# A hybrid decoder layer: the first head pair's half projections as three per attention step, and the memory's 1/rms operations at a higher priority

## The chip, the cores and the metric

The kernel runs on one core of a Trainium2 chip. The metric is device time in microseconds of one execution, as the median of several runs. The engines named below are PE (the matrix engine, with PEld for its weight loads), DVE (the vector engine), ACT (the scalar engine), POOL (the general engine) and SP (which here only issues DMA transfers).

## The reference

One layer of a causal decoder is computed for a batch of 1, 512 tokens and a model width of 1024, in float32. Only the mixer sublayer's attention and the memory's RMSNorm matter here:

```python
h = rms_norm(x, norm_mix[l])
proj = h @ w_in[l]
q_a, k_a, v_a, u_b, gate_b, gate_c, g_a, g_b = jnp.split(proj, split_points, axis=-1)
...
z = jnp.einsum('bhqd,bhkd->bhqk', qb, kb) * scale
log_fail = jnp.where(mask, jax.nn.log_sigmoid(-z), 0.0)
log_later = lax.cumsum(log_fail, axis=3, reverse=True) - log_fail
weights = jnp.where(mask, jnp.exp(jax.nn.log_sigmoid(z) + log_later), 0.0)
outs.append(jnp.einsum('bhqk,bhkd->bhqd', weights, vb))
...
y_b = gate_b * causal_depthwise_conv(gate_c * u_b, conv_w[l])
merged = jax.nn.sigmoid(g_a) * branch_a + jax.nn.sigmoid(g_b) * branch_b
x = x + merged @ w_mix_out[l]
x = x + memory_cross_attention(rms_norm(x, norm_mem_q[l]), rms_norm(mem, norm_mem_kv[l]), ...)
```

The stick-breaking attention has 8 heads of 64 channels. A weight of key s for query t is a sigmoid times a product over the keys between them, so each score tile needs a sum over all later keys before its exponential can be taken. After the mixer come the cross-attention into 256 memory tokens, a SwiGLU sublayer and a last RMSNorm.

## The kernel before, in words

Every float32 operand of a matmul is split into a high part, rounded to the matmul's own format, and a low part. A product takes three matmuls: high by high, high by low, low by high (`mm3`, lines 155 to 157). A weight tile is loaded by SP (`wr`, line 143), cast by ACT to its high part (`wh`, line 150) and subtracted by DVE to its low part (`wl`, line 151). There are four buffers each of `wr`, `wh` and `wl`.

The input projection is computed in column blocks of 128. One block is a projection of 8 chunks of the model width, 24 matmuls of 128x512 into one PSUM bank `pr`. It is cut in two halves of 12 matmuls each, `open_project` and the rest in `project`, and after the second half DVE evicts the bank: `qk_part` for queries and keys (L294), `conv` for the convolution branch (`gc` L315, `cu` L321 and L322, `cv` L324 and L328, `gb` L334 and L335) and `gate` for the merge gates (L307). The pool of these banks (`pmm`) has two.

The attention works on pairs of heads p = 0 to 3, and for each pair on key tiles kt = 3, 2, 1, 0, each with all queries from its own on. That makes 16 steps, numbered 0 to 15 in the text, with 128, 256, 384 and 512 queries for two heads. For one step

- `scores` makes z = q.k on PE (L382 or L389), then ACT takes |z|, exp and log (L396 to L398), DVE adds max(z, 0) to make e (L399), and POOL clears what lies above the diagonal (L355);
- `parts` adds on DVE the carry, the sum over later tiles (L420), and splits e into high and low, `l`, by ACT (L369) and DVE (L370);
- `weights` adds with PE the running sum of both parts onto z by a triangular matrix (`negtri`, L433); then DVE takes the next carry from row 0 of z (L438), which SP copies from partition 0 to partition 127 (L444), ACT takes the exponential `a` (L441), POOL clears its diagonal block, and DVE splits it into `ah` and `al` (L449, L450);
- `values` multiplies by v on PE (L461).

The loop over steps runs one step ahead with the scores: iteration i computes some half projections, then the scores of step i+1, then `weights` of step i, which wait for the second `l` of step i, and then `values` of step i-1. So the half projections of an iteration are the work on PE under which ACT, DVE and POOL bring z of step i to `l`. How many of the 44 halves an iteration takes is set by the table `FILL`: its first row gives the shares of pair 0's four steps, its second row those of each other pair, and `fill_some` takes halves until the cumulated share is reached. The order of the 44 is fixed: queries and keys of the next pair, then gc, u and gb of the convolution, pair by pair, and at the end four merge gates. Before, the shares sum to 44, so the iterations take 3, 2, 3, 3 halves and then 2, 2, 3, 4 for each of the other three pairs.

The order of PE's work is the order of the code. On ACT, DVE, POOL and SP a list scheduler sets the order at build time by the code's order and by priorities: `tc.high_priority(n)` lets the operations inside it count as written n places earlier. The attention's own chain uses 100 and 150.

The squares of the memory are summed on the way. In iteration 14 two small products with a constant (`var`, L188, ahead of the scores; `varb`, L197, after the values) give its mean square by token and along the free axis, each in a bank of `pmm`, and `rstd_of` makes 1/rms of each, `rm` and `rmb`, with operations on ACT (L121, L126, L127) and DVE (L124, L128, L129, L131). They are needed much later, at `km` and `vm`.

Of the kernel before, what the change touches and what calls it, by code (L numbers as in the profile page):

```python
# [29 lines left out]
MEM_AT = (5, 7, 9, 11)  # L30
MEAN_AT = 14
EARLY = 2
FILL = ((3, 2, 3, 3), (2, 2, 3, 4))
WARM = 8
FIRST = 4

# [4 lines left out]
def hybrid_layer(ctx: ExitStack, tc: tile.TileContext, xT_d, memT_d, cols_d, wv_d, win_d,  # L41
# [135 lines left out]
    def squares_mean(acc, n):  # L177

        parts = unit("acch", n * P), unit("accl", n * P)
        nc.vector.tensor_copy(parts[0], acc)  # L180
        nc.vector.tensor_tensor(out=parts[1], in0=acc, in1=f(parts[0]), op=ALU.subtract)

        def by_token(s, tables=(), bank=otile):

            vp = bank("var")
            for t in range(n):
                for i in range(2):
                    nc.tensor.matmul(vp[:, 2 * t:2 * t + 2], parts[i][:, t * P:(t + 1) * P],  # L188
                                     mean_r[:, 0:2], start=i == 0, stop=i == 1)
            return rstd_of(vp[:, 0:2 * n].rearrange("p (t two) -> p t two", two=2)[:, :, 0], n, s,  # L190
                           tables)

        def along(s, tables=(), bank=otile, keep=None):

            vp = bank("varb")[:, :n * P]
            for i in range(2):
                nc.tensor.matmul(vp, mean_r, parts[i], start=i == 0, stop=i == 1)  # L197
            return rstd_of(vp, n * P, s, tables, keep=keep)

        return by_token, along  # L200
# [103 lines left out]
    def gate(m, j):  # L304
        ps = project((O_A, O_B)[j] + m * P)
        t = gates[m, j] = tmp("g")
        nc.vector.tensor_tensor(out=t, in0=ps, in1=r0b, op=ALU.mult)  # L307
# [65 lines left out]
    def scores(p, kt):  # L373
        c0, n = span(kt)
        q, k = qk[p]
        ks = slice(kt * P, (kt + 1) * P)
        terms = (0, 0), (0, 1), (1, 0)
        if 2 * n <= 512:
            zs[p, kt] = [ztile("z")[:, :2 * n]]
            z3 = by_head(zs[p, kt], kt)[0]  # L380
            for i, (a, b) in enumerate(terms):
                nc.tensor.matmul(z3, k[a][:, ks], late_q[p % 2][b][:, :, c0 - HS:],  # L382
                                 start=i == 0, stop=i == 2)
        else:
            zs[p, kt] = [ztile("z")[:, :n] for _ in range(2)]
            for i, (a, b) in enumerate(terms):
                for h in range(2):
                    hs = slice(h * HD, (h + 1) * HD)
                    nc.tensor.matmul(zs[p, kt][h], k[a][hs, ks], q[b][hs, c0:],  # L389
                                     start=i == 0, stop=i == 2)  # L390
        es[p, kt] = []
        with tc.high_priority(100):
            for h, z in enumerate(zs[p, kt]):
                w = z.shape[1]
                e = tmp("e")[:, :w]
                nc.scalar.activation(e, z, AF.Abs)  # L396
                nc.scalar.activation(e, e, AF.Exp, scale=-1.0)
                nc.scalar.activation(e, e, AF.Ln, bias=1.0)  # L398
                nc.vector.scalar_tensor_tensor(out=e, in0=z, scalar=0.0, in1=e, op0=ALU.max,  # L399
                                               op1=ALU.add)  # L400
                causal(by_head([e], kt)[0])
                es[p, kt].append(e)
                if kt > 0:
                    r = carries[kt % 2][0:1, h * w:(h + 1) * w]
                    first.setdefault((p, kt), []).append(r)
                    nc.scalar.copy(r, z[0:1, :])

    def parts(p, kt):


        c0, n = span(kt)
        sp[p, kt] = []
        with tc.high_priority(100):
            for h, e in enumerate(es.pop((p, kt))):
                w = e.shape[1]
                if kt < TT - 1:
                    c = carries[(kt + 1) % 2][P - 32:P, h * w // n * (n - P):]
                    c = c[:, :w // n * (n - P)].rearrange("p (h n) -> p h n", n=n - P)
                    e3 = e.rearrange("p (h n) -> p h n", n=n)[P - 32:P, :, P:]
                    nc.vector.tensor_tensor(out=e3, in0=e3, in1=c, op=ALU.add)  # L420
                sp[p, kt].append(lsplit(e, w, f"l{kt % 2}"))
# [6 lines left out]
    def weights(p, kt):  # L428
        c0, n = span(kt)
        av[p, kt] = []  # L430
        for z, both in zip(zs[p, kt], sp[p, kt]):
            for part in both:
                nc.tensor.matmul(z, negtri, part, start=False, stop=True, skip_group_check=True)  # L433
        exp_a = []
        got = first.get((p, kt), [])
        with tc.high_priority(150):
            for r, z in zip(got, zs[p, kt]):
                nc.vector.tensor_tensor(out=r, in0=r, in1=z[0:1, :], op=ALU.subtract)  # L438
            for h, z in enumerate(zs[p, kt]):
                exp_a.append(tmp("a")[:, :z.shape[1]])  # L440
                exps.append(nc.scalar.activation(exp_a[h], z, AF.Exp))  # L441
            for h, r in enumerate(got):
                w = r.shape[1]
                nc.sync.dma_start(carries[kt % 2][P - 1:P, h * w:(h + 1) * w], r)  # L444
        for a in exp_a:
            causal(by_head([a], kt)[0])
            w = a.shape[1]
            ah, al = unit("ah")[:, :w], unit("al")[:, :w]
            nc.vector.tensor_copy(ah, a)  # L449
            nc.vector.tensor_tensor(out=al, in0=a, in1=f(ah), op=ALU.subtract)  # L450
            for i in range(w // n):
                av[p, kt].append((ah[:, i * n:(i + 1) * n], al[:, i * n:(i + 1) * n]))

    def values(p, kt):
        c0 = span(kt)[0]
        if kt == TT - 1:
            ops[p] = [otile("o") for _ in range(2)]
        for h in range(2):
            w = v[kt][h][:, p, :, :]
            for i in range(2):  # L460
                nc.tensor.matmul(ops[p][h][:, c0:], w, av[p, kt][h][i],  # L461
                                 start=kt == TT - 1 and i == 0, stop=kt == 0 and i == 1,
                                 skip_group_check=True)
        if kt == 0:

            t = tmp("ot")
            for h in range(2):
                hs, other = (slice(j * HD, (j + 1) * HD) for j in (h, 1 - h))
                nc.scalar.copy(t[hs, :], ops[p][h][other, :])
                nc.vector.tensor_tensor(out=t[hs, :], in0=ops[p][h][hs, :], in1=t[hs, :],  # L470
                                        op=ALU.add)
            oT.append(split(t, "o"))
# [7 lines left out]
    def mem_square(k2):  # L480

        mk = f(unit("mk")).rearrange("p (j t) -> p j t", j=2)
        load_mem(k2, mk)
        nc.scalar.activation(accm if k2 == 0 else mk, mk, AF.Square)
        if k2 > 0:
            nc.vector.tensor_tensor(out=accm, in0=accm, in1=mk, op=ALU.add)
        if k2 == KD // 2 - 1:
            nc.vector.tensor_tensor(out=accm[:, 0, :], in0=accm[:, 0, :], in1=accm[:, 1, :],
                                    op=ALU.add)
# [16 lines left out]
    n_fill = len(fill)  # L506
    shares = FILL[0] + (TT - 1) * FILL[1]

    def fill_some(to):
        while fill and n_fill - len(fill) < to:  # L510
            g, *args = fill.pop(0)
            g(*args)
# [5 lines left out]
    with tc.manual_schedule(engines={mybir.EngineType.PE}):  # L518
        for i in range(len(steps) + 1):
            if i in MEM_AT:  # L520
                mem_square(MEM_AT.index(i))
            if i == MEAN_AT - 2:
                mean = squares_mean(accm[:, 0, :], MT)
            fill_some(n_fill * sum(shares[:i + 1]) / sum(shares))
            if i == MEAN_AT:
                rm = mean[0]("rm", bank=mmtile)
            if i + 1 < len(steps):
                scores(*steps[i + 1])
            if i < len(steps):
                weights(*steps[i])  # L530
            else:
                gate(EARLY, 0)
            if i + 1 < len(steps):
                parts(*steps[i + 1])
            if i > 0:
                values(*steps[i - 1])
            if i == MEAN_AT:
                rmb = mean[1]("rmb", bank=mmtile)

    stick.close()  # L540
    xpool = ctx.enter_context(tc.tile_pool(name="xpool", bufs=8))
# [552 lines left out]
```

## Time and profile before

| | us |
|---|---|
| median of 3 runs | 861.33 |
| lowest and highest of them | 860.83, 861.85 |
| the profiled execution's own time | 860.98 |
| its span | 859.2 |
| PE busy | 850.5 |
| DVE busy | 586.5 |
| ACT busy | 431.1 |
| POOL busy | 62.0 |

Times in rows are counted from the span's start. A row of the timeline gives the start, the duration, the engine, the line, the operation, out<-in and how many instructions are merged; in brackets stands how long the engine had been idle before and what released it. Matmuls overlap in the pipeline, so a 128x512 one shows a duration of about 0.39 us while the next starts some 0.23 us after it; lengths of PE's work are therefore taken from start to start. The same is done for DVE, whose rows overlap by under 0.1 us.

### The profile page before, as it was taken

The page shows a single profiled execution, that of the slowest core. Times are in us where ns is not written, and L with a number is a line of the kernel's source. Part 1 is how long each engine was busy: PE and PEld are TensorE (multiplying, and loading weights), DVE is VectorE, ACT ScalarE, POOL GpSimd, SP SyncE. Part 2 cuts the span into 40 slices and gives each one's busy share as a digit, 9 for nine tenths or more (in the row PEclk, how much of TensorE's full clock was granted, in tenths as well). Part 3 has the DMA queues.
Part 4 walks back from the last instruction along what each step waited for, and adds up shares of the span by engine and source line. Part 5 has one row for each costly group of instructions (what it writes and reads, how often), then busy time and mean ns, then how long its engine had stood idle before and what let it go on. Part 6 is the DMA issues. An engine that isn't in the chain of part 4 may idle for free.

```text
span 859.2 us, 12693 instructions
## 1 busy us (share of the span) xinstructions
PE 850.5 (99%) x4912; PEld 748.6 (87%) x4912; DVE 586.5 (68%) x963; ACT 431.1 (50%) x750; POOL 62.0 (7%) x92
## 2 busy tenths in 40 slices
PE   9999999999999999999999999999999999999997
PEld 7877788888888898888888889999999999888897
DVE  8769898986454475555555779888887778533334
ACT  7566766665333344433444666555445556422335
POOL 1011111111000000000000101111111100000002
PEclk9999999999999999999999999999999999999999
DMA  8322331228333255422110527776777753322202
GB/s 295 132 90 77 120 111 62 74 99 266 111 103 111 96 177 184 143 98 98 50 67 33 137 54 202 187 182 172 185 188 195 182 147 127 119 98 99 73 1 98
DMA packets 42859, 108.34 MB, mean 126 GB/s; under 512 B 4656, under 2 KB 8752, under 8 KB 42800
## 3 DMA queue, kind: packets, MB, share of 16 engines
q1 hardware_dynamic: 36528, 95.72, 32.8%
q0 software_dynamic: 5984, 11.54, 8.2%
q8 instruction: 38, 0.62, 0.3%
q10 hardware_dynamic: 288, 0.29, 0.1%
q14 instruction: 21, 0.17, 0.1%
HBM read 104.36 MB, written 2.10 MB: 124 GB/s over the span
## 4 chain that ended last, share of the span: by engine, by line
PE 96%; DVE 2%; DMA 1%; issue 0%; POOL 0%; SPq 0%; DVEq 0%; ACT 0%; POOLq 0%
PE z L801 15%; PE y L801 7%; PE pr L155 7%; PE pr L156 7%; PE pr L157 7%; PE f L156 5%; PE f L157 5%; PE f L155 5%; PE v L801 4%; PE r L156 3%; PE r L155 3%; PE r L157 3%; PE v L261 3%; PE mq L156 2%; PE mq L157 2%; PE mq L155 2%
## 5 line engine op out<-in xcount | busy, mean ns | idle before, releaser
L150 ACT CAST wh<-wr 128x1024 fp32r<-128x1024 f32 x106 | 111.1, 1050 | 222.2 <-issue 98.6
L151 DVE TENSOR_TENSOR wl<-wr,wh 128x1024 fp32r<-128x1024 f32 x106 | 129.4, 1223 | 99.4 <-ACT wh L150 99.2
L155 PE MATMUL pr<-xgh,wh 128*128 128x512 f32 x288 | 112.6, 391 | 0.0
L156 PE MATMUL pr<-xgl,wh 128*128 128x512 f32 x288 | 112.4, 390 | 0.0
L157 PE MATMUL pr<-xgh,wl 128*128 128x512 f32 x288 | 112.3, 390 | 0.0
L156 PE MATMUL f<-actl,wh 128*128 128x512 f32 (+1 forms) x208 | 74.3, 357 | 0.0
L155 PE MATMUL f<-acth,wh 128*128 128x512 f32 (+1 forms) x208 | 74.2, 357 | 0.0
L157 PE MATMUL f<-acth,wl 128*128 128x512 f32 (+1 forms) x208 | 74.1, 357 | 0.0
L801 PE MATMUL z<-xdh,wf 128*128 128x256 f32 x352 | 70.4, 283 | 0.0
L157 PEld LDWEIGHTS pr<-xgh,wl 128*128 128x128 f32 x288 | 54.1, 188 | 11.3
L155 PEld LDWEIGHTS pr<-xgh,wh 128*128 128x128 f32 x288 | 54.1, 188 | 10.9
L156 PEld LDWEIGHTS pr<-xgl,wh 128*128 128x128 f32 x288 | 54.1, 188 | 10.8
L758 POOL DMA_DIRECT2D ws<-in_w_ffn_in_dram x22 | 26.6, 1208 | 469.0 <-DVE c L616 267.8
L801 PEld LDWEIGHTS z<-xdh,wf 128*128 128x128 f32 x352 | 58.0, 192 | 0.0
L821 ACT COPY sa<-z 128x256 f32<-128x256 f32 x44 | 16.4, 372 | 78.3 <-PE z L801 78.2
L801 PE MATMUL z<-xdl,wf 128*128 128x256 f32 x176 | 49.9, 283 | 0.0
L792 DVE TENSOR_TENSOR wf<-s,wf 128x512 fp32r<-128x512 f32 x44 | 30.3, 691 | 21.1 <-ACT wf L791 20.0
L155 PEld LDWEIGHTS f<-acth,wh 128*128 128x128 f32 x208 | 39.3, 189 | 5.8
L156 PEld LDWEIGHTS f<-actl,wh 128*128 128x128 f32 x208 | 39.3, 189 | 5.6
L157 PEld LDWEIGHTS f<-acth,wl 128*128 128x128 f32 x208 | 39.3, 189 | 5.5
L801 PE MATMUL v<-xoh,wf 128*128 128x256 f32 x176 | 35.5, 283 | 0.0
L801 PE MATMUL y<-xch,wf 128*128 128x256 f32 x176 | 35.5, 283 | 0.0
(281 smaller groups left out, 2134.8 us busy)
## 6 DMA issues: line engine op xcount, KB each, us to landing
wr<-in_w_in_dram SPq DMA_DIRECT2D x36, 512.0 KB, 3.3
ws<-in_w_ffn_in_dram SPq DMA_DIRECT2D x22, 512.0 KB, 3.8
wg<-in_w_ffn_in_dram SPq DMA_DIRECT2D x22, 512.0 KB, 4.2
ws<-in_w_ffn_in_dram POOLq DMA_DIRECT2D x22, 512.0 KB, 5.8
wr<-in_w_ffn_out_dram SPq DMA_DIRECT2D x22, 512.0 KB, 3.3
a<-in_w_ffn_in_dram SPq DMA_DIRECT2D x22, 256.0 KB, 4.5
wr<-in_w_branch_dram SPq DMA_DIRECT2D x8, 512.0 KB, 3.2
wr<-in_w_mem_k_dram SPq DMA_DIRECT2D x8, 512.0 KB, 3.2
```

The costliest lines, as they stand in the source:

```text
L150: after(nc.scalar.copy(h2, raw), lead[-1:])
L151: lows.append(nc.vector.tensor_tensor(out=l2, in0=raw, in1=f(h2), op=ALU.subtract))
L155: nc.tensor.matmul(ps, a[0], b[0], start=start, stop=False, **kw)
L156: nc.tensor.matmul(ps, a[0], b[1], start=False, stop=False, **kw)
L157: nc.tensor.matmul(ps, a[1], b[0], start=False, stop=stop, **kw)
L261: nc.tensor.matmul(vps[t], xg[k][a][:, sl], wv[k][b], start=k == 0 and (a, b) == (0, 0), stop=k == KD - 1 and a == 1)
L758: nc.gpsimd.dma_start(s13, a[:, 0:4:3, :], accum_op=ALU.add)
L792: nc.vector.tensor_tensor(out=lo, in0=raw, in1=f(hi), op=ALU.subtract)
L801: nc.tensor.matmul(ps[:, :HS], a, b, start=i < 3 and k == 0 and j == 0, stop=k == KP - 1 and j == 2, skip_group_check=True)
L821: nc.scalar.copy((s[:, :HS], None, None, s[:, HS:], t[:, :HS])[i], z)
```

## The change

Two things change. The first row of `FILL` becomes (3, 3, 3, 3). The shares then sum to 45 for the same 44 halves, so the iterations take 3, 3, 3, 3, then 2, 2, 3, 4 twice, and for the last pair 2, 2, 3, 3: from iteration 1 to iteration 14 one half more has been done than before, and iteration 15 has one less. And the operations of `rm` and `rmb` get a priority as if written 150 places earlier. No instruction's shape or count changes.

```diff
-FILL = ((3, 2, 3, 3), (2, 2, 3, 4))
+FILL = ((3, 3, 3, 3), (2, 2, 3, 4))
...
             fill_some(n_fill * sum(shares[:i + 1]) / sum(shares))
             if i == MEAN_AT:
-                rm = mean[0]("rm", bank=mmtile)
+                with tc.high_priority(150):
+                    rm = mean[0]("rm", bank=mmtile)
             if i + 1 < len(steps):
                 scores(*steps[i + 1])
...
             if i == MEAN_AT:
-                rmb = mean[1]("rmb", bank=mmtile)
+                with tc.high_priority(150):
+                    rmb = mean[1]("rmb", bank=mmtile)
```

PE around iteration 1, before: the scores of step 2 (L389) and the weights of step 1 (L433) follow the first half of the projection `pr_607`, whose halves end with wl rows; xgh_177 is the fourth chunk of eight.

```order
L157 MATMUL pr_607<-xgh_177,wl_604 128x512
L389 MATMUL z_620<-qkh_434,qkh_475 128x384
L389 MATMUL z_621<-qkh_434,qkh_475 128x384
L389 MATMUL z_620<-qkl_435,qkh_475 128x384
L389 MATMUL z_621<-qkl_435,qkh_475 128x384
L389 MATMUL z_620<-qkh_434,qkl_476 128x384
L389 MATMUL z_621<-qkh_434,qkl_476 128x384
L433 MATMUL z_556<-l_579,negtri 128x512
L433 MATMUL z_556<-l_580,negtri 128x512
```

PE at the same place after the change; xgh_217 is the last chunk.

```order
L157 MATMUL pr_607<-xgh_217,wl_604 128x512
L389 MATMUL z_634<-qkh_434,qkh_475 128x384
L389 MATMUL z_635<-qkh_434,qkh_475 128x384
L389 MATMUL z_634<-qkl_435,qkh_475 128x384
L389 MATMUL z_635<-qkl_435,qkh_475 128x384
L389 MATMUL z_634<-qkh_434,qkl_476 128x384
L389 MATMUL z_635<-qkh_434,qkl_476 128x384
L433 MATMUL z_556<-l_579,negtri 128x512
L433 MATMUL z_556<-l_580,negtri 128x512
```

The second half of `pr_607`, 12 matmuls, now stands ahead of these scores and weights.

DVE between the evictions of the convolution's u and the weights of step 3, before.

```order
L438 TENSOR_TENSOR carry_397<-carry_397,z_620 1x384
L438 TENSOR_TENSOR carry_397<-carry_397,z_621 1x384
L324 TENSOR_SCALAR cv_718<-cu_714,gcol 128x512
L328 SCALAR_TENSOR_TENSOR cv_718<-cu_714,gcol,cv_718 128x512 x2
L449 CAST ah_755<-a_748 128x384
L450 TENSOR_TENSOR al_756<-a_748,ah_755 128x384
L449 CAST ah_760<-a_750 128x384
L450 TENSOR_TENSOR al_761<-a_750,ah_760 128x384
L399 SCALAR_TENSOR_TENSOR e_730<-z_722,e_730 128x512
L399 SCALAR_TENSOR_TENSOR e_736<-z_723,e_736 128x512
L420 TENSOR_TENSOR e_730<-e_730,carry_397 32x384
L420 TENSOR_TENSOR e_736<-e_736,carry_397 32x384
```

DVE at the same place after the change.

```order
L324 TENSOR_SCALAR cv_718<-cu_714,gcol 128x512
L328 SCALAR_TENSOR_TENSOR cv_718<-cu_714,gcol,cv_718 128x512 x2
L438 TENSOR_TENSOR carry_397<-carry_397,z_634 1x384
L438 TENSOR_TENSOR carry_397<-carry_397,z_635 1x384
L449 CAST ah_774<-a_767 128x384
L399 SCALAR_TENSOR_TENSOR e_749<-z_741,e_749 128x512
L450 TENSOR_TENSOR al_775<-a_767,ah_774 128x384
L449 CAST ah_779<-a_769 128x384
L420 TENSOR_TENSOR e_749<-e_749,carry_397 32x384
L399 SCALAR_TENSOR_TENSOR e_755<-z_742,e_755 128x512
L450 TENSOR_TENSOR al_780<-a_769,ah_779 128x384
L420 TENSOR_TENSOR e_755<-e_755,carry_397 32x384
```

The convolution's `cv` now stands ahead of the carries, and step 3's first e is no longer behind both splits of step 2's weights.

DVE ahead of the weights of step 15, before; `rv`, `ra` and `rmb` belong to 1/rms along the free axis, and g_1993 is the eviction of a merge gate.

```order
L124 TENSOR_SCALAR rv_1952<-varb_1949 128x256
L399 SCALAR_TENSOR_TENSOR e_1907<-z_1894,e_1907 128x512
L420 TENSOR_TENSOR e_1901<-e_1901,carry_397 32x384
L420 TENSOR_TENSOR e_1907<-e_1907,carry_397 32x384
L450 TENSOR_TENSOR al_1932<-a_1921,ah_1931 128x384
L370 TENSOR_TENSOR l_1937<-e_1901,l_1936 128x512
L128 TENSOR_TENSOR ra_1954<-ry_1953 128x256
L370 TENSOR_TENSOR l_1942<-e_1907,l_1941 128x512
L129 SCALAR_TENSOR_TENSOR ra_1954<-ra_1954,rv_1952 128x256
L307 TENSOR_TENSOR g_1993<-pr_1968,r0b_338 128x512
L131 SCALAR_TENSOR_TENSOR rmb_1955<-ra_1954,ry_1953 128x256
```

DVE at the same place after the change.

```order
L124 TENSOR_SCALAR rv_1971<-varb_1968 128x256
L399 SCALAR_TENSOR_TENSOR e_1920<-z_1912,e_1920 128x512
L450 TENSOR_TENSOR al_1951<-a_1940,ah_1950 128x384
L399 SCALAR_TENSOR_TENSOR e_1926<-z_1913,e_1926 128x512
L128 TENSOR_TENSOR ra_1973<-ry_1972 128x256
L420 TENSOR_TENSOR e_1920<-e_1920,carry_397 32x384
L129 SCALAR_TENSOR_TENSOR ra_1973<-ra_1973,rv_1971 128x256
L420 TENSOR_TENSOR e_1926<-e_1926,carry_397 32x384
L131 SCALAR_TENSOR_TENSOR rmb_1974<-ra_1973,ry_1972 128x256
L370 TENSOR_TENSOR l_1956<-e_1920,l_1955 128x512
L307 TENSOR_TENSOR g_1993<-pr_1884,r0b_338 128x512
L370 TENSOR_TENSOR l_1961<-e_1926,l_1960 128x512
```

All of the 1/rms operations and the gate's eviction now stand ahead of the second `l`, on which the weights of step 15 wait; and `rv`, which frees the bank of `varb`, stands ahead of step 15's first e.

## The prediction

> **What bounds the kernel.** The page comes first. PE is busy for 99% of the span and makes 96% of the chain that ended last, so only time in which PE stands still can be won, since the change takes no matmul away.
>
> ```profile
> PE 850.5 (99%) x4912; PEld 748.6 (87%) x4912; DVE 586.5 (68%) x963; ACT 431.1 (50%) x750; POOL 62.0 (7%) x92
> PE 96%; DVE 2%; DMA 1%; issue 0%; POOL 0%; SPq 0%; DVEq 0%; ACT 0%; POOLq 0%
> ```
>
> Then comes the list of who waited for whom, for PE. In the attention PE waits for one thing only, the second `l` of a step, made by DVE at L370.
>
> ```profile
> PE z L433 <- DVE l L370: 0.9, 2, 0.5
> ```
>
> Ends of matmuls are modelled, so 0.9 us is a lower bound. The timeline of PE gives the whole of it, from start to start: a step that waits against one of the same shape that doesn't.
>
> ```profile
> 55.07 0.44 PE L389 MATMUL z<-qkh,qkh 64*128 64x384 f32 x2
> 56.72 0.50 PE L433 MATMUL z<-l,negtri 128*128 128x512 f32 x1 [0.43 <-DVE l L370]
> 57.45 0.45 PE L155 MATMUL pr<-xgh,wh 128*128 128x512 f32 x1
> 65.78 0.50 PE L389 MATMUL z<-qkh,qkh 64*128 64x512 f32 x2
> 76.15 0.40 PE L382 MATMUL z<-lq,qkh 128*128 128x256 f32 x2
> 77.99 0.50 PE L433 MATMUL z<-l,negtri 128*128 128x512 f32 x1 [0.47 <-DVE l L370]
> 79.03 0.39 PE L155 MATMUL pr<-xgh,wh 128*128 128x512 f32 x1
> ...
> 115.02 0.40 PE L382 MATMUL z<-lq,qkh 128*128 128x256 f32 x2
> 116.99 0.39 PE L155 MATMUL pr<-xgh,wh 128*128 128x512 f32 x1
> 129.89 0.44 PE L389 MATMUL z<-qkh,qkh 64*128 64x384 f32 x2
> 131.56 0.45 PE L155 MATMUL pr<-xgh,wh 128*128 128x512 f32 x1
> ```
>
> Iteration 1 takes 57.45 - 55.07 = 2.38 us from its scores to its next projection, iteration 9 with the same work 131.56 - 129.89 = 1.67: 0.71 us are waited. Iteration 3 takes 79.03 - 76.15 = 2.88, iteration 7 takes 116.99 - 115.02 = 1.97: 0.91 us. So 1.62 us, 0.19% of the time, is what the first part of the change can win. One half projection is worth (65.78 - 57.45) / 3 = 2.78 us there.
>
> **Iteration 1: a third half.** The `l` for which iteration 1 waits, and the DVE work that makes convolution and e for step 3, stand in these rows of DVE's timeline.
>
> ```profile
> 55.98 0.68 DVE L370 TENSOR_TENSOR l<-e,l 128x512 fp32r<-128x512 f32 x1
> ...
> 65.89 0.69 DVE L321 TENSOR_TENSOR cu<-pr,r0b 128x512 f32<-128x512 f32 x1 [1.22 <-PE pr L157]
> ...
> 68.36 1.00 DVE L438 TENSOR_TENSOR carry<-carry,z 1x384 f32<-1x384 f32 x2
> ...
> 69.79 1.54 DVE L328 SCALAR_TENSOR_TENSOR cv<-cu,gcol,cv 128x512 f32<-128x512 f32 x2
> ...
> 72.98 1.28 DVE L399 SCALAR_TENSOR_TENSOR e<-z,e 128x512 f32<-128x512 f32 x2
> 74.29 1.12 DVE L420 TENSOR_TENSOR e<-e,carry 32x384 f32<-32x384 f32 x2
> ...
> 77.25 0.68 DVE L370 TENSOR_TENSOR l<-e,l 128x512 fp32r<-128x512 f32 x1
> ```
>
> `l` ends at 55.98 + 0.68 = 56.66, and nothing ahead of it on DVE, ACT or SP is moved. The scores of iteration 1 now start at 55.07 + 2.78 = 57.85, and the weights after them. `l` is ready 1.2 us before even the scores, so the wait goes whole: -0.71. From here on everything of the attention runs 2.78 - 0.71 = 2.07 us later, with one half more done.
>
> **Iteration 3: the same three halves, but an earlier convolution.** Here the chain of work runs on DVE without a pause: u's eviction at 65.89, the convolution, both e's, both `l`'s, to 77.25 + 0.68 = 77.93. Now u's projection ends one half earlier against the scores. DVE is then free of step 2's `l` at about 65.9 (an estimate from its rows, within 1 us), so the convolution starts at the same clock time as before, while the scores of step 3 come at 65.78 + 2.07 = 67.85. The convolution without the carries ends at 69.79 + 1.54 - 1.00 = 70.3 and the two carries (L438, 1.00) behind it at 71.3. The next limit is SP's transfer of the carry:
>
> ```profile
> DMA to landing us min/median/max: 1.6/2.8/3.8
> ```
>
> The second transfer is issued about 0.6 after the first. It lands at 71.3 + 0.6 + 2.8 = 74.7, between 73.5 and 75.7. From the second carry's addition (74.29 + 0.56 = 74.85) to the second `l`'s end took 77.93 - 74.85 = 3.08 before, with gb's eviction in it, which is still there. So `l` is ready at 77.8, at the latest at 78.8. The last matmul of the weights stood at 77.99 with a wait of 0.91, so without one it is due at 77.08 + 2.07 = 79.15. It is early by 0.3 to 2.6: the wait goes, -0.91. Its bounds are 0 and -0.91; I take the whole, since even the slowest landing shown leaves it.
>
> On SP the loads of weights move by one half with the projections, and step 4's carry now stands behind one more load and the copies of pair 2's queries. That load waits for a `wl` that DVE makes ahead of the same carry, so I cost it at nothing; what hides it is DVE's order, and if the load's buffer came later, step 5 would wait. POOL gets the same selects; one fill of 2 columns is moved ahead of two of them.
>
> **Iterations 5 and 13: tight before.** The second `l` here ends just ahead of the weights.
>
> ```profile
> 91.14 0.68 DVE L370 TENSOR_TENSOR l<-e,l 128x512 fp32r<-128x512 f32 x1
> 91.74 0.69 DVE L170 TENSOR_TENSOR ol<-ot,oh 128x512 fp32r<-128x512 f32 x1
> ...
> 167.89 0.68 DVE L370 TENSOR_TENSOR l<-e,l 128x512 fp32r<-128x512 f32 x1
> ```
>
> ```profile
> 92.64 0.73 PE L433 MATMUL z<-l,negtri 128*128 128x512 f32 x2
> 168.57 0.73 PE L433 MATMUL z<-l,negtri 128*128 128x512 f32 x2
> ```
>
> In iteration 5, 92.64 - 91.82 = 0.82 us were spare. Now the split `ol` (0.69) stands ahead of `l`: 0.13 are left. I add 0.1, with bounds of 0 and 0.7 (the whole of `ol` again, if ACT's part of it is late). In iteration 13 nothing was spare (167.89 + 0.68 = 168.57), and gb's eviction, which stood between the carry's addition and `l`, now comes ahead of e: I cost it at nothing.
>
> **Iterations 14 and 15: one half less, and 1/rms first.** These rows are DVE's and PE's between the memory's product and the weights of step 15.
>
> ```profile
> 183.49 0.41 DVE L124 TENSOR_SCALAR rv<-varb 128x256 f32<-128x256 f32 x1
> 184.53 1.12 DVE L420 TENSOR_TENSOR e<-e,carry 32x384 f32<-32x384 f32 x2
> 185.68 0.56 DVE L450 TENSOR_TENSOR al<-a,ah 128x384 fp32r<-128x384 f32 x1
> ...
> 186.75 0.42 DVE L128 TENSOR_TENSOR ra<-ry 128x256 f32<-128x256 f32 x1
> 187.09 0.69 DVE L370 TENSOR_TENSOR l<-e,l 128x512 fp32r<-128x512 f32 x1
> 187.69 0.42 DVE L129 SCALAR_TENSOR_TENSOR ra<-ra,rv 128x256 f32<-128x256 f32 x1
> 188.03 0.69 DVE L307 TENSOR_TENSOR g<-pr,r0b 128x512 f32<-128x512 f32 x1
> 188.63 0.42 DVE L131 SCALAR_TENSOR_TENSOR rmb<-ra,ry 128x256 f32<-128x256 f32 x1
> 188.96 1.22 DVE L151 TENSOR_TENSOR wl<-wr,wh 128x1024 fp32r<-128x1024 f32 x1
> ```
>
> ```profile
> 180.61 0.40 PE L155 MATMUL pr<-xgh,wh 128*128 128x512 f32 x1
> 191.52 0.87 PE L433 MATMUL z<-l,negtri 128*128 128x512 f32 x3
> ```
>
> The four halves ran from 180.61 to 191.52, 2.73 us each. The second `l` was ready at 187.78, 3.74 early. With three halves all up to 180.61 comes 2.73 later against the weights: 1.01 left. The third matmul of the weights, the one that needs it, is due 0.46 after the first, at 191.98. From `rv`'s start to the second `l`'s end DVE took 187.78 - 183.49 = 4.29. Now one of e's L399 (half of 1.28, 0.64) comes behind `rv` instead of ahead, and 0.34 (L129), 0.60 (the gate's eviction) and 0.33 (L131) come ahead of `l`: 6.20. `rv` itself starts 0.64 earlier, at 183.49 + 2.73 - 0.64 = 185.58. So `l` ends at 191.78, 0.2 early. The priority of `rmb` is thus no gift: its 0.67 us lie ahead of the chain. The cost is 0 by this sum; the other end comes from POOL's select between e and its carry:
>
> ```profile
> 46.87 1.49 POOL L355 TENSOR_SCALAR_AFFINE_SELECT e<-e 128x256 f32<-128x256 f32 x1 [42.21 <-DVE e L399]
> 52.15 0.53 POOL L355 TENSOR_SCALAR_AFFINE_SELECT e<-e 128x256 f32<-128x256 f32 x1 [1.00 <-DVE e L399]
> ```
>
> The same select took 1.49 us beside other work on DVE and 0.53 elsewhere. An extra 0.96 here would make a wait of 0.76. I take 0.1. [...]
>
> A bank is also shared anew. The merge gate begun in iteration 14 now holds one of the two `pmm` banks, so `var`, `varb` and the next gate's projection all use the other. That projection is due when the first of the three halves ends, 180.61 + 2 x 2.73 = 186.07, and `rv` has read `varb` at 185.58 + 0.41 = 185.99. Bounds 0 and 0.6 (L399 in front of `rv` after all); I take 0.1. `rm`'s three operations on 2 columns are each shorter than `rmb`'s 0.42 and hidden under iteration 14's halves; without that cover they would cost under 1.3.
>
> **The sum.** -0.71 - 0.91 + 0.1 + 0.1 + 0.1 = -1.3. The profiled execution took 860.98, 0.35 under the median of 861.33; against it the sum gives 859.7, against the median 860.0. What can be told from no change is 0.2%, 1.72 us: under 859.61 or over 863.05.
>
> **The rivals.** First, the waits move: DVE is the engine behind every `l`, and its work per pair is unchanged. For it speaks that iterations 5, 13 and 15 have under 1 us to spare; against it, that iteration 13 had nothing to spare and its row shows no idle time. If iteration 3 keeps its wait and the new ones come in full, the change is -0.71 + 0.76 + 0.7 + 0.6 = +1.35, 862.7; midway between this and the forecast, 861.3. Chance 0.22. Second, the end on the other side: the hand-over of `varb`'s bank. PE stands in iteration 15 until ACT and DVE have read it. It decides if `rv` ends 3.0 us after the 186.07 at which it is due, which makes +1.7, 863.1 and more. No row shows ACT or DVE that late there. Chance 0.06. Third, more than the two waits: spread between runs (860.83 to 861.85) on top of the full 1.62, for 859.5. Chance 0.18. A change that does nothing, 861.3, would need iteration 1's wait to stay although a whole half is put ahead of it; it is part of the first rival.
>
> **How the numbers follow.** The forecast, both waits gone and up to 0.6 given back, has 0.54, and its time is 860.0. Under 859.61 lies the third rival (0.18), over 863.05 the second (0.06), the rest, 0.76, is within 0.2%. The range reaches from 859.2 (the full 1.62 and half of the spread) to 862.2 (most of the first rival).
>
> **What will show it.** Right: no wait of PE's L433 for L370 in iterations 1 and 3, 1.67 and 1.97 us from scores to projection there, and the attention's end 1.0 to 1.6 us earlier. Wrong: a new idle time ahead of L433 in iterations 5 or 15, or ahead of `pr` in iteration 15 with ACT's L121 or DVE's L124 as releaser. Work behind the attention should only be shifted.

## The result, and the profile after

The changed kernel takes 859.65 us as the median of 15 executions (859.25 to 860.47). The kernel before, run beside it 15 times, takes 861.27 (860.11 to 861.91). The ratio is 0.9984 with an interval of 0.9977 to 0.9991: 1.62 us less, which is clear of the spread between executions, but within the 0.2% that the forecast had set as what can be told from no change. The forecast was 860.0, and the line under which it left the field to its third rival was 859.61, only 0.04 below what was measured. The profiled execution has its own time of 859.25 and a span of 857.5.

The page of the changed kernel, its engines and the chain that ended last:

```profile
PE 850.1 (99%) x4912; PEld 748.4 (87%) x4912; DVE 585.9 (68%) x963; ACT 430.7 (50%) x750; POOL 64.5 (8%) x92
PE 99%; DVE 0%; POOL 0%; issue 0%; DVEq 0%; ACT 0%; POOLq 0%
```

DVE and DMA have dropped out of the chain: 2% and 1% before, 0% and no entry now. The list of who waited for whom has a single row left for PE, the wait for the warm-up matmuls' operand before the attention. The row for L433 and L370 is gone.

```profile
PE warm L220 <- DVE neg L87: 1.6, 1, 1.6
```

PE's timeline of iterations 1 and 3, which waited before (scores, weights, next projection):

```profile
57.49 0.44 PE L389 MATMUL z<-qkh,qkh 64*128 64x384 f32 x2
58.21 0.73 PE L433 MATMUL z<-l,negtri 128*128 128x512 f32 x2
59.16 0.45 PE L155 MATMUL pr<-xgh,wh 128*128 128x512 f32 x1
...
77.86 0.40 PE L382 MATMUL z<-lq,qkh 128*128 128x256 f32 x2
78.22 1.09 PE L433 MATMUL z<-l,negtri 128*128 128x512 f32 x4
79.84 0.39 PE L155 MATMUL pr<-xgh,wh 128*128 128x512 f32 x1
```

Iteration 1 takes 59.16 - 57.49 = 1.67 us, iteration 3 takes 79.84 - 77.86 = 1.98: the times that iterations 9 and 7 had before. All four weight matmuls of iteration 3 now run as one group, with no wait among them.

The tight places, DVE and then PE: iteration 3's and iteration 5's second `l`, and iteration 15.

```profile
74.70 0.56 DVE L420 TENSOR_TENSOR e<-e,carry 32x384 f32<-32x384 f32 x1
...
76.50 0.68 DVE L370 TENSOR_TENSOR l<-e,l 128x512 fp32r<-128x512 f32 x1
...
91.95 0.69 DVE L170 TENSOR_TENSOR ol<-ot,oh 128x512 fp32r<-128x512 f32 x1
92.58 0.69 DVE L370 TENSOR_TENSOR l<-e,l 128x512 fp32r<-128x512 f32 x1
...
183.72 0.42 DVE L124 TENSOR_SCALAR rv<-varb 128x256 f32<-128x256 f32 x1
...
187.79 0.42 DVE L131 SCALAR_TENSOR_TENSOR rmb<-ra,ry 128x256 f32<-128x256 f32 x1
188.14 0.68 DVE L370 TENSOR_TENSOR l<-e,l 128x512 fp32r<-128x512 f32 x1
188.74 0.68 DVE L307 TENSOR_TENSOR g<-pr,r0b 128x512 f32<-128x512 f32 x1
189.34 0.68 DVE L370 TENSOR_TENSOR l<-e,l 128x512 fp32r<-128x512 f32 x1
```

```profile
93.45 0.73 PE L433 MATMUL z<-l,negtri 128*128 128x512 f32 x2
...
181.42 0.40 PE L155 MATMUL pr<-xgh,wh 128*128 128x512 f32 x1
...
184.20 0.50 PE L155 MATMUL pr<-xgh,wh 128*128 128x512 f32 x1
...
189.79 1.10 PE L433 MATMUL z<-l,negtri 128*128 128x512 f32 x4
```

- Iteration 3: `l` ends at 77.18, 1.04 ahead of the first weight matmul at 78.22.
- Iteration 5: `l` ends at 93.27, 0.18 ahead of the weights at 93.45, with `ol` in front of it.
- Iteration 15: `l` ends at 190.02. The third matmul of the weights, which needs it, is due at 189.79 + 0.46 = 190.25: 0.23 early.
- The bank that `varb` used: `rv` has read it at 184.14, and the second of iteration 15's three halves, which takes the bank, starts at 184.20, 2.78 after the first instead of 2.73. That half itself takes 2.86, since its second matmul starts 0.33 behind its first instead of 0.23. So the three halves take 189.79 - 181.42 = 8.37 instead of 3 x 2.73 = 8.19, 0.18 more. PE's weight loads show the wait:

```profile
PEld pr L155 <- DVE rv L124: 0.3, 1, 0.3
```

From the attention's first projection (28.66 before, 28.32 after) to the first matmul of the merge's `br` (199.55 and 197.82) it took 170.89 us before and 169.50 after: 1.39 less. The other 0.34 lies ahead of the attention, whose start moves between 28.3 and 29.5 from one profile to another. Nothing ahead of it was changed, so this part is no gain of the change.

### The profile page after: what moved, and what is told of

The parts are those of the page before. It is cut to its first block, busy times and chain, and to the rows that moved or that the text cites. A ratio compares the mean times of both kernels' runs of the same rounds, so it can differ in the third digit from the quotient of the medians.

```text
span 857.5 us, 12690 instructions
## 1 busy us (share of the span) xinstructions
PE 850.1 (99%) x4912; PEld 748.4 (87%) x4912; DVE 585.9 (68%) x963; ACT 430.7 (50%) x750; POOL 64.5 (8%) x92
## 4 chain that ended last, share of the span: by engine, by line
PE 99%; DVE 0%; POOL 0%; issue 0%; DVEq 0%; ACT 0%; POOLq 0%
PE z L803 15%; PE pr L155 8%; PE pr L156 8%; PE pr L157 8%; PE y L803 7%; PE f L156 5%; PE f L155 5%; PE f L157 5%; PE v L803 4%; PE r L157 3%; PE r L156 3%; PE r L155 3%; PE v L261 3%; PE mq L157 2%; PE mq L155 2%; PE mq L156 2%
```

## The experiments

All are edits of the changed kernel, apart from the second part alone, where the old shares stand. "Attention" is the length just defined, in the profiled execution; the ratio is to the kernel before, run on the same chip. The kernel before took 861.33 beside the shares alone, the priority alone, the half moved from iteration 15 to 3 and the mean in iteration 15; 861.0 beside the two repeated kernels ("again") and priority 110; 860.93 beside the others.

| kernel | median us | ratio, 95% interval | attention us |
|---|---|---|---|
| before | 861.27 | 1 | 170.89 |
| changed | 859.65 | 0.9984, 0.9977 to 0.9991 | 169.50 |
| shares alone | 864.42 | 1.0039, 1.0026 to 1.0051 | 173.93 |
| shares alone, again | 864.36 | 1.0040, 1.0026 to 1.0054 | 174.05 |
| priority alone | 861.13 | 1.0001, 0.9992 to 1.0010 | 170.63 |
| half moved from iteration 15 to 3 only | 860.13 | 0.9989, 0.9980 to 0.9998 | 170.29 |
| mean in iteration 15 | 859.80 | 0.9985, 0.9976 to 0.9994 | 169.39 |
| priority 100 | 861.83 | 1.0020, 1.0011 to 1.0029 | 171.40 |
| priority 100, again | 861.33 | 1.0007, 0.9998 to 1.0015 | 171.39 |
| priority 110 | 860.42 | 0.9993, 0.9985 to 1.0002 | 170.08 |
| half moved from iteration 2 to 1 | 860.76 | 0.9999, 0.9990 to 1.0007 | 170.49 |
| four halves first | 860.89 | 0.9997, 0.9989 to 1.0006 | 171.05 |
| four halves first, mean in iteration 15 | 860.84 | 0.9999, 0.9990 to 1.0008 | 170.33 |

### The shares alone

```diff
             if i == MEAN_AT:
-                with tc.high_priority(150):
-                    rm = mean[0]("rm", bank=mmtile)
+                rm = mean[0]("rm", bank=mmtile)
...
             if i == MEAN_AT:
-                with tc.high_priority(150):
-                    rmb = mean[1]("rmb", bank=mmtile)
+                rmb = mean[1]("rmb", bank=mmtile)
```

> The new shares without the higher priority. Theory A, both parts belong together: the waits of iterations 1 and 3 go (-1.62), but rv, which frees the bank of varb, now stands on DVE behind both of step 15's e's and both carry additions (two L399, one L450, two L420, some 2.9 us in the changed kernel's rows) instead of ahead of them. It would end near 187.0 on the changed kernel's clock, while PE wants the bank at 184.2: a wait of about 2.7 us ahead of pr in iteration 15, and a time of +1.0 against before, 862.3. Rival B, the shares do it all and the priority is no gift, as the prediction's sum has it: -1.6 to -1.3, 859.7 to 860.0, with no wait ahead of pr over 0.6 us.

Both waits of iterations 1 and 3 are gone here too (1.67 and 1.98), and the kernel is 0.39% slower than before. PE has one new wait, and its timeline shows where:

```profile
PE pr L155 <- DVE rv L124: 2.9, 1, 2.9
```

```profile
184.69 0.39 PE L157 MATMUL pr<-xgh,wl 128*128 128x512 f32 x1
188.03 0.80 PE L155 MATMUL pr<-xgh,wh 128*128 128x512 f32 x1 [2.95 <-DVE rv L124]
188.62 0.63 PE L156 MATMUL pr<-xgl,wh 128*128 128x512 f32 x1
189.05 0.63 PE L157 MATMUL pr<-xgh,wl 128*128 128x512 f32 x1
```

DVE, at the same place: `rv` stands behind the last carry addition of the next step.

```profile
186.96 0.56 DVE L420 TENSOR_TENSOR e<-e,carry 32x384 f32<-32x384 f32 x1
187.55 0.42 DVE L124 TENSOR_SCALAR rv<-varb 128x256 f32<-128x256 f32 x1
```

The place and the length are those of theory A, which had put the idle at 2.7; the price is not, +3.1 for +1.0. The rest of it is in the windows of PE (us, PE busy, granted clock, DMA share, GB/s):

```profile
185.00:188.00 3.00, 0.08 (x1) 0.94 0.00 0
188.00:190.00 2.00, 1.97 (x5) 0.50 0.03 8
190.00:191.00 1.00, 1.00 (x4) 0.50 0.00 0
191.00:193.00 2.00, 2.00 (x10) 0.99 0.00 0
```

Behind the idle the granted clock is 0.50 for about 3 us, and matmuls start 0.43 us apart (188.62 to 189.05) instead of 0.23. The mean of 0.94 over the three us before 188 says that the fall came some 0.4 us before 188 (0.06 x 3 / 0.50), while PE still stood; in all the half clock lasts some 3.4 us, an estimate from these rows. The three halves take 12.80 instead of 8.19, 4.6 more. Some 3.3 of that are the idle with its edges: with priority 100 and 110 below, the halves grow by 0.3 more than the idle. The idle is counted from the shown end of a matmul of 0.39, where the next otherwise starts after 0.23, and from the first matmul behind it to the second it takes 0.34 (186.10 to 186.44 with priority 100). The other 1.4 are the seven matmuls behind the idle, which take 3.08 here (188.03 to 191.11) and 1.73 with priority 100 (186.10 to 187.83). Rival B, that the priority is only a cost, falls: without it the change is 864.42 - 861.33 + 1.62 = 4.7 us worse.

### The priority alone

```diff
-FILL = ((3, 3, 3, 3), (2, 2, 3, 4))
+FILL = ((3, 2, 3, 3), (2, 2, 3, 4))
```

> The higher priority with the old shares. Theory A: no merge gate is open across the memory's products and the second l of step 15 has 3.7 us to spare, so nothing changes: 0.0, within 0.3, and the waits of iterations 1 (0.71) and 3 (0.91) stay. Rival B, the priority is worth time of its own because 1/rms stands in the way of later work: -0.3 or more.

No change by the time, and PE's row of waits is still there:

```profile
PE z L433 <- DVE l L370: 0.7, 2, 0.5
```

Iterations 1 and 3 take 2.12 and 2.88. In iteration 15 the second `l` is 2.10 us early instead of 3.74: the 1/rms operations do stand in front of it, and with four halves as cover that costs nothing. (Both are counted to the first of the weights' matmuls.) Iteration 1's wait, 0.45 here and 0.71 in the profile before, differs from profile to profile although nothing around it was changed. The two parts of the change thus only pay together: the shares make the waits go and open the new one at the bank, and the priority closes that.

### One half moved past iteration 3 only

```diff
-FILL = ((3, 3, 3, 3), (2, 2, 3, 4))
+FILL = ((3, 2, 3, 4), (2, 2, 3, 4))
```

> First row of shares 3, 2, 3, 4: the half is added in iteration 3 instead of iteration 1, all else from iteration 4 on as in the changed kernel. Theory A, each wait has its own price: iteration 1 keeps 0.71, iteration 3 loses 0.91, so it lies 0.7 above the changed kernel, -0.9 against before, about 860.4. Rival B, one half more anywhere ahead of iteration 4 does the same: -1.6.

Iteration 3 takes 1.97, iteration 1 still waits:

```profile
56.65 0.51 PE L433 MATMUL z<-l,negtri 128*128 128x512 f32 x1 [0.55 <-DVE l L370]
```

Iteration 1 takes 57.38 - 54.89 = 2.49, so 0.82 are waited in this profile, and the attention is 0.79 longer than with the change. The half added in iteration 3 takes iteration 3's wait away and leaves iteration 1's, which is theory A. The medians alone would not decide it: 1.2 below the kernel before lies between theory A's 0.9 and rival B's 1.6.

### The memory's mean one iteration later

```diff
-MEAN_AT = 14
+MEAN_AT = 15
```

> The changed kernel with the memory's products one iteration later, where no merge gate is open and DVE has no scores to serve. Theory A: the wait ahead of pr in iteration 15 (0.18 us from start to start) goes and the second l of step 15 has 1 to 2 us to spare instead of 0.2: -0.2 against the changed kernel, -1.8 against before. Rival B, what is put on DVE and PE behind step 15 delays its values or the next gate: +0.2 or more against the changed kernel.

`varb` is then made after the halves of iteration 15 and shares no bank with them. PE's timeline, first of iteration 15's three halves, then `var` behind them and the weights; and DVE's last `l`:

```profile
181.91 0.40 PE L155 MATMUL pr<-xgh,wh 128*128 128x512 f32 x1
...
190.09 0.17 PE L188 MATMUL var<-mean_r,acch 128*128 128x2 f32 x1
...
190.46 1.18 PE L433 MATMUL z<-l,negtri 128*128 128x512 f32 x4
```

```profile
189.95 0.68 DVE L370 TENSOR_TENSOR l<-e,l 128x512 fp32r<-128x512 f32 x1
```

The three halves take 190.09 - 181.91 = 8.18: the 0.19 at the bank is gone. The margin did not grow, though. `l` ends at 190.63, 0.29 before the weights' third matmul at 190.46 + 0.46, because a gate's eviction (0.69 at 188.21) and a `wl` (1.22 at 188.82) took the 1/rms operations' place on DVE. The attention is 0.11 shorter; the time can't be told from that of the change, so neither theory is decided by it, and theory A's margin of 1 to 2 us did not come.

### Lower priorities: 100 and 110

```diff
-                with tc.high_priority(150):
+                with tc.high_priority(100):
```

at both places, and likewise with 110. Priority 100 puts two of e's additions (L399) and a carry's addition ahead of `rv`, priority 110 one L399.

> The changed kernel with a priority of 100 instead of 150. rv now stands behind one carry addition and both L399 of step 15 on DVE, but ahead of the second carry addition: by the rows of the run with the shares alone it ends at about 186.8 there instead of 187.98, so PE idles ahead of pr in iteration 15 for about 1.8 us instead of 2.95. Theory A, an idle time costs its own length and the extra 1.5 us of the run with the shares alone came from the lower granted clock after it, which needs a longer idle time than this: -1.57 + 1.8 = +0.2 against before, 861.5, and a granted clock of 1.00 behind the wait. Rival B, any idle time of PE of over 1 us lowers the clock: +1.5 more, 863.0, with matmuls 0.43 apart behind the wait.

PE is idle for 1.77 us ahead of the second half in iteration 15, and the three halves take 10.26, 2.07 more than 8.19. In the profiled execution the granted clock behind the idle is 1.00:

```profile
184.00:186.00 2.00, 0.34 (x2) 1.00 0.00 0
186.00:187.00 1.00, 0.90 (x4) 1.00 0.07 16
```

So in this execution only the idle was paid, as theory A had it, though 0.9 instead of 0.2 by the median. The 11 times explain most of that: six lie from 861.1 to 861.8 with a mean granted clock of 0.998 to 1.0 over the span, five from 863.4 to 863.9 with 0.997. This, and one execution of five of the shares alone that took 862.5 at 0.999 where the others took 864.4 to 864.9 at 0.996 to 0.997, led to the next three runs.

> The kernel of the run with priority 100 once more. There, PE's idle of 1.77 us in iteration 15 left the granted clock of the profiled execution at 1.00, but the times fell in two groups: six from 861.1 to 861.8 with a mean clock of 0.998 to 1.0, five from 863.4 to 863.9 with 0.997. Theory A: after such an idle the clock is halved for about 3 us in a part of the executions, as the idle falls against something that is not of this kernel. Then the two groups come again, some 2 us apart, the later with a mean clock 0.001 to 0.002 lower, and where the profiled execution is of the later group, its rows behind the idle show matmuls 0.43 us apart and a clock of 0.50. Rival B: the halving needs an idle longer than 1.77 us and the later group has another cause (loads from HBM). Then a profile of the later group shows the clock at 1.00 behind the idle and the time lost elsewhere.

This time one of 11 executions took 863.6, at 0.997, and ten 861.1 to 861.7, at 0.998 to 1.0. The profiled one was of the ten, and shows the same 1.77 of idle with matmuls 0.23 apart behind it. So the idle's own price is known, 1.9 of attention over the change. The two groups came again, as theory A had it, but no profile is of the later group, so its cause was not seen, nor anything outside the kernel against which the idle would fall.

> The kernel with the new shares and no priority once more; idle of 2.95 us. In the first run four executions took 864.4 to 864.9 at a mean clock of 0.996 to 0.997, one 862.5 at 0.999. Theory A: the idle is always there and costs about +1.2 against before (862.1 to 862.5); the halved clock, +2 more, comes in most executions but not in all. Both groups show again, and the earlier has a profile, if it is the profiled one, with the wait and 0.23 us from matmul to matmul behind it. Rival B: the halving belongs to an idle of this length; all executions take 864 or more.

All five executions took 864.0 to 865.2 at 0.996 to 0.997, and the profile has again the 2.95 of idle and matmuls 0.43 apart behind it. With the run before, nine of ten executions lost the further 2 us. Neither text is right as it stands: a mean clock of 0.996 or 0.997 came in nine of the ten executions, but not in each. The earlier group, the one at 0.999, has no profile.

> Changed kernel with priority 110 instead of 150 on the 1/rms operations: one of e's additions (L399, 0.60 us apart on DVE) stands ahead of rv, not two and a carry's addition as with 100. PE's idle ahead of the second half in iteration 15 should be 0.4 to 0.7 us. Theory A: the idle costs its own length, about +0.5 on the changed kernel's 859.65, 860.2, and its times form one group, or nearly so. Rival B: any idle can halve the clock; then a part of the executions takes 861.5 to 862.5 with a mean clock 0.001 lower.

```profile
185.42 0.50 PE L155 MATMUL pr<-xgh,wh 128*128 128x512 f32 x1 [0.47 <-DVE rv L124]
```

An idle of 0.47, three halves in 8.96 (0.77 more than 8.19), attention 0.58 longer than with the change, one group of times from 859.9 to 861.1 at 0.998 to 1.0. That is theory A. The table of the idle ahead of that half is then:

| idle in the profiles, us | three halves, us | executions at a mean clock of 0.997 or less |
|---|---|---|
| none shown (priority 150) | 8.37 | 0 of 15 |
| 0.47 (110) | 8.96 | 0 of 11 |
| 1.77 (100) | 10.26 | 6 of 22 |
| 2.95 (no priority) | 12.80 | 9 of 10 |

Of the 66 executions of the experiments' other six kernels, and of those of the kernel before, none has a mean clock under 0.998.

### A half moved from iteration 2 to iteration 1

```diff
-FILL = ((3, 3, 3, 3), (2, 2, 3, 4))
+FILL = ((3, 3, 2, 3), (2, 2, 3, 4))
```

> First row of shares 3, 3, 2, 3, sum 44: iteration 1's half is taken from iteration 2, and iteration 15 keeps its four. Theory A: iteration 1's wait goes (-0.71); iteration 2 had 3.15 us to spare with three halves in the changed kernel, so with two it still has 0.4 and does not wait; the convolution's u ends where it did against step 3's scores, so iteration 3 keeps its 0.91: -0.7 against before, 860.6. Rival B, the waits only move: iteration 2 waits for what iteration 1 no longer does, 0.0.

The sum of the shares is 44 again, iteration 15 keeps four halves, and only iteration 1 gets a third. Its wait goes (1.68), iteration 2 has none (its margin is 0.39, as expected), but iteration 3 waits longer:

```profile
75.36 0.40 PE L382 MATMUL z<-lq,qkh 128*128 128x256 f32 x2
...
77.50 0.50 PE L433 MATMUL z<-l,negtri 128*128 128x512 f32 x1 [0.47 <-DVE l L370]
78.54 0.39 PE L155 MATMUL pr<-xgh,wh 128*128 128x512 f32 x1
```

It takes 78.54 - 75.36 = 3.18, 1.21 of wait for 0.91 before. The attention gains 0.40 of the 0.7. DVE's rows ahead of it show why:

```profile
64.47 1.03 DVE L370 TENSOR_TENSOR l<-e,l 128x384 fp32r<-128x384 f32 x2 [0.30 <-ACT l L369]
65.41 0.68 DVE L321 TENSOR_TENSOR cu<-pr,r0b 128x512 f32<-128x512 f32 x1
```

The eviction of the convolution's u, which begins the chain to step 3's second `l`, stands right behind step 2's `l` and starts 0.42 after the scores of step 3 (64.99). Before it started 0.11 after them (65.89 for 65.78). From there to the end of the second `l` DVE takes 12.03 us here and 12.04 before, so the 0.3 of later start are the 0.3 of longer wait. Here the first rival of the prediction, waits that move, is at work.

### Four halves first

```diff
-FILL = ((3, 3, 3, 3), (2, 2, 3, 4))
+FILL = ((4, 3, 3, 3), (2, 2, 3, 4))
```

> First row of shares 4, 3, 3, 3: iteration 0 takes a fourth half, iteration 7 gives one up. Theory A: the wait inside iteration 0's weights (0.35 us from start to start against iteration 4) goes, iteration 7 had 3.5 us to spare in the changed kernel and keeps 0.7, so 0.35 less than the changed kernel, -1.9 against before, 859.4. Rival B: iteration 5, which had 0.2 us to spare, or iteration 7 waits by more than 0.35, and it is not faster than the changed kernel.

Iteration 0's short wait goes (0.93 for 1.28), and iteration 3's comes back (3.20 for 1.98). PE's row, and DVE's ahead of it:

```profile
82.81 0.50 PE L433 MATMUL z<-l,negtri 128*128 128x512 f32 x1 [0.69 <-DVE l L370]
```

```profile
78.83 0.56 DVE L420 TENSOR_TENSOR e<-e,carry 32x384 f32<-32x384 f32 x1 [1.25 <-DMA carry<-carry]
...
81.47 0.68 DVE L294 SCALAR_TENSOR_TENSOR qk<-pr,r0b 128x512 f32<-128x512 f32 x1
82.07 0.68 DVE L370 TENSOR_TENSOR l<-e,l 128x512 fp32r<-128x512 f32 x1
```

DVE stands 1.25 us for the carry's transfer, and a projection's eviction (L294) comes in front of the second `l`. Iterations 7 and 12 also wait, 0.43 and 0.22 by their lengths. That is rival B.

```diff
-MEAN_AT = 14
+MEAN_AT = 15
...
-FILL = ((3, 3, 3, 3), (2, 2, 3, 4))
+FILL = ((4, 3, 3, 3), (2, 2, 3, 4))
```

> Both, the fourth half in iteration 0 and the memory's products in iteration 15. Theory A: the two gains add, 0.35 + 0.1 to 0.2 below the changed kernel, -2.0 against before, 859.3. Rival B: the places are tied by DVE's order and one gain is given back, -1.6.

Iteration 3 takes 2.73 and iteration 7 2.50. The gains don't add, as rival B had it, but even its -1.6 was too much: 860.84 is 0.1 below the kernel before. Neither version is faster than before by its interval, and none of the kernels run is faster than the change.

## Why the prediction was right, point by point

| term of the sum | predicted | measured |
|---|---|---|
| iteration 1's wait | -0.71 | -0.71 (2.38 to 1.67) |
| iteration 3's wait | -0.91 | -0.90 (2.88 to 1.98) |
| iteration 5 | +0.1, 0.13 spare | 0, 0.18 spare |
| iteration 13 | 0, nothing spare | 0, 1.13 spare |
| iteration 15, second `l` | +0.1, 0.20 early | 0, 0.23 early |
| hand-over of `varb`'s bank | +0.1 | +0.18 |
| sum | -1.3 | -1.39 in the attention, -1.62 by the medians |

- **The two waits** went whole and stayed gone. The profile after shows it, and the kernels that take away only one of them show it one by one. The size of iteration 1's is less sure than the table looks: with the same work it was 0.71, 0.45 and 0.82 in three profiles.
- **Iteration 3** came out right, but its last limit was another than the one worked out. The text had the second carry's transfer as limit, at a landing of 2.8 us. Both transfers of this step landed in 1.7, the second at about 72.5 (issued at 70.75), and the second carry addition stood behind DVE's own work until 74.70, with no idle time ahead of it. `l` was 1.04 ahead of the first weight matmul where the working had 0.66 (79.15 - 0.69 - 77.8).
- **Iterations 5 and 15** came out within 0.05 of the margins worked out from DVE's rows. POOL's select, whose slow row was the upper bound there, didn't slow down: the two ahead of step 15's `l` took 0.55 and 0.41. They are of 128x128, while the slow row was of 128x256, so the bound was of another shape. Nor do the rows of before show that DVE's work is what slows it: beside the select of 1.49 DVE made a `wl` (1.23 at 46.88), beside the one of 0.53 an `al` (0.42 at 52.00) and a projection's eviction (0.69 at 52.46). In iteration 13 gb's eviction did come ahead of e: `l` ended at 168.26 and the weights began at 169.39.
- **The bank** was the only new cost. Its upper bound, 0.6 with one L399 in front of `rv`, is what priority 110 makes; the halves measured 0.77 more there (8.96 for 8.19), the idle and its edges.
- **The first rival**, waits that move, did not come about with this change: the only new idle time at a place it named is the bank's. It was real nearby, as the kernels with a half taken from iteration 2 and with four halves first show.
- **The second rival** was no far-off case but one edit away. Its mechanism, its place and its 3.0 us of lateness are what the shares alone do (2.95). Its price of +1.7 was short by 1.4 (the shares alone cost 3.1), since the sum took the idle at its own length and left out its edges and the clock of 0.50 behind it.
- **The third rival**, more than the two waits, can't be told from the forecast by the medians alone: 859.65 lies nearer to its 859.5 than to 860.0. What speaks for the forecast is the profile, with both waits gone, 0.18 given back and an attention that is 1.39 shorter. That the medians came out at the full 1.62 is then luck.
- **Where the text was wrong in substance** though not in the number is the sentence that the priority of `rmb` "is thus no gift". For the second `l` that is so. With the shares alone it ends 160.57 us after the attention's start (188.95 + 0.69 - 29.07), with the change 161.70 (190.02 - 28.32): the priority makes it 1.13 later. But the same working took `rv`'s early place, which the priority gives, as a fact of the bank's term, and never priced the kernel without it. The priority is worth 4.7 us, three times what the waits are.
- **The 0.23 left over** between the attention's 1.39 and the medians' 1.62 is not explained; the attention's start alone moves by 1.2 us between profiles.

## What to carry to other kernels

When a table of work shares takes filler away from one place to put it at another, look at the place that loses it for resources that the filler was also hiding: here a PSUM bank of a pool of two, read late by low-priority operations on DVE. A wait of PE is to be priced with the clock that the windows of a profile show behind it: here an idle of 0.47 us cost 0.6 to 0.8, one of 2.95, with a granted clock of 0.50 behind it, 4.4 to 4.6. Price each part of a change also without the other; a part that looks like a mere cost may be what the gain of the other hangs on.

## What the runs showed of the hardware

In the first profile of the shares alone the granted TensorE clock fell to 0.50 around the end of an idle of 2.95 us and stayed there for about 3 us of PE's work (0.50 from 188 to 191, 0.99 from 191 to 193), with 128x512 matmuls 0.43 us apart instead of 0.23. The second profile has the same idle, and behind it matmuls 0.43 apart from 188.76 to 190.90. It was not a matter of the kernel alone: of ten executions of that kernel nine show a mean clock of 0.996 or 0.997 over the span and one 0.999, and of 22 of the kernel with an idle of 1.77 six show 0.997 and a time some 2 us later than the others. Half a clock for 3 us of 863 is 0.0017 of the mean, which fits these means. That the six lost their time behind the idle is argued from that, and not shown, since neither profile was of one of them; half a clock for 3.4 us would also cost only 1.7 of their some 2 us.
